# Two more expert pairs scattered, the last two summed in PSUM, low parts in pieces, and 512-column projections in a two-layer hybrid decoder kernel

## The chip, the cores and the metric

One core of a Trainium2 chip. The metric is the device time of one execution in microseconds (us), the median of three runs. TensorE (PE) multiplies matrices, VectorE (DVE), ScalarE (ACT) and GpSimd (POOL) work element by element, SyncE (SP) issues most DMA transfers. SBUF is the memory on the chip, PSUM the small one into which PE writes.

## What is computed

Two layers over 528 tokens (16 learned meta tokens and 512 of the input), 1024 features. Each layer has a mixer (four heads of a gated delta rule beside sparse attention with a token indexer), a residual norm, a mixture of experts (32 experts, two per token), and a second norm. Cut from the reference:

```python
for l in range(DEPTH):
    proj = h @ w_in[l]
    dq, dk, dv, dz, db, da, sq, sk, sv, iq, ik, iw = jnp.split(proj, SPLIT_POINTS, axis=-1)
    o_dn = deltanet_group(dq, dk, dv, dz, db, da, ...)       # short convolution of 4 taps on q, k, v first
    o_sa = dsa_group(sq, sk, sv, iq, ik, iw, ...)            # per query the top keys by the indexer
    mix = jnp.concatenate([o_dn, o_sa], axis=-1) @ w_out[l]
    h = layer_norm(DEEPNORM_ALPHA * h + mix, ln1_g[l], ln1_b[l])
    ffn = hier_moe(h, ...)                                   # top group of 4, then 2 of its 8 experts
    h = layer_norm(DEEPNORM_ALPHA * h + ffn, ln2_g[l], ln2_b[l])
```

where `hier_moe` sums, over a token's two experts, gate x (silu(t w1) * (t w3)) w2.

## The kernel before, in words

The order in which each engine issues its instructions is fixed ahead of the run by the framework's list scheduler, from the program and a model of its costs; `tc.issue_after(x)` only keeps an instruction behind x. So a change in one place can move instructions everywhere.

**Projections.** Activations and weights are split into a high and a low part, and a projection is high x high + low x high + high x low: 24 products of 128 weight columns each, accumulated in one PSUM bank. `project` (L314) does the tokens in two halves of 264 columns, or of 256 where the meta tokens are left out (`c0` = 16): the index queries of both layers, and in layer 1 the attention queries, the gates and the output projection. `between` runs after the first half. `weights` (L213) loads 512 KB, ACT copies the high part and POOL subtracts the low part (L186, 1024 columns; every other weight of the output projection on DVE). The low parts share a tag with four buffers, the high parts one with two.

**Convolution.** The first of four taps is on POOL (L513), the other three on DVE (L515). `att_values` copies transposed values on DVE (L900).

**Experts.** 16 pairs of experts, 64 rows for each expert. For each pair: `gather` (L1234, POOL) fetches its tokens' rows by an indirect DMA, `transpose_rows` (L1362) transposes them on PE (xtq) and scales them on ACT and DVE into xT, in two halves; `expert_hidden` (L1308) makes h in 32 products; `expert_out` (L1323) makes the output yp in two halves of 8 products in the banks of `po_` and `pa`. For pairs 0 to 11 (`SENT` = 12, L49), `gated_rows` stores gate x yp into yw (ACT one half, L1349, DVE the other, L1350), and POOL scatters its rows into the table ytab in device memory (L1481). yw shares the high parts' two buffers, so a store waits for the scatter of two pairs before. For pairs 12 to 15, `gated` (L1340) stores a high part yw (ACT) and a low part yl (DVE), and `combine` (L1377) places the rows by products with a 0/1 matrix G (two per half tile of 128 tokens) and adds them on DVE (L1397) to the residual h. `todo` and `advance` (L1399 to L1403) spread the combinations of pairs 12 to 14 over the pairs that follow; those of pair 15 are in the tail.

**Weights of the experts** are six transfers of 1 MB per pair on SP's queue (`load_pair`, L309).

**Tail.** At pair 15, behind the vectors of the second norm (lnw), `fetch_rows` (L1416) loads the table's rows (yr) into the buffers of `unit`. A branch for experts with more than 64 tokens follows (`tc.If`, L1501; not taken here). Behind it `norm_stats` (L1598) does for each tile: `merge_rows` (L1431: two adds of the table's rows to h on DVE, L1434), the combination of pair 15, with the sum for the mean (on DVE, L1395, or, in the mode "e", on ACT with h itself added by a product with the identity), then variance and norm.

## Time and profile before

| | us |
|---|---|
| median of three runs | 1503.27 (1502.39 to 1503.33) |
| profiled execution | 1504.99 |
| its span, first to last instruction | 1503.2 |
| PE busy | 1312.8 |
| DVE busy | 882.5 |
| POOL busy | 588.1 |
| ACT busy | 528.4 |
| mean granted TensorE clock | 0.937 of full speed |

Layer 0's mixer takes until about 476, its experts until 735, its tail until 775; layer 1's mixer until 1217, its experts until 1470, the tail to the end. Times in the profile count from the start of the span. A busy PE includes waiting inside a pipelined run of products; what an instruction costs PE is therefore read from one start to the next. An idle time in brackets names what the profile found to have come last.

### The profile page before, as it was taken

The numbers are of one execution on the slowest core, as the hardware profiler recorded it, in microseconds if no ns is written. First come the engines' busy times: TensorE is split into PE (matmuls) and PEld (weight loads), VectorE is DVE, ScalarE is ACT, GpSimd is POOL, SyncE is SP. The second block draws the span as 40 slices with busy tenths as digits, with TensorE's granted clock in tenths as the row PEclk, the third lists the DMA queues.
The fourth block names the chain that finished last, engine by engine and source line by source line (L and its number), as shares of the span: only waits on it lengthen the run. The fifth ranks groups of instructions, "written<-read, shape, count | busy, mean of one in ns | idle before, by whom it ended". The sixth has DMA issues, their size and how long they took to land. (4 is left out here: it accounts for less than half of the span.)

```text
span 1503.2 us, 25678 instructions
## 1 busy us (share of the span) xinstructions
PE 1312.8 (87%) x9592; PEld 958.3 (64%) x9592; DVE 882.5 (59%) x2151; ACT 528.4 (35%) x1385; POOL 588.1 (39%) x581
## 2 busy tenths in 40 slices
PE   7898998799996898779778989988999879978794
PEld 7898998787894332223368989988888733322231
DVE  5898999656446131113788888998573341311157
ACT  3454544245322222222134544442453222221212
POOL 3665497626013211210146664878340231211102
PEclk9999999869997999999889999999799989999997
DMA  5252133122626999999432521222236379999971
GB/s 174 79 183 75 53 91 89 62 72 110 260 82 254 406 409 359 410 410 380 154 108 73 186 73 60 79 70 66 100 140 253 106 299 410 409 409 410 409 305 56
DMA packets 103121, 305.59 MB, mean 203 GB/s; under 512 B 24248, under 2 KB 25352, under 8 KB 102992
## 3 DMA queue, kind: packets, MB, share of 16 engines
q1 hardware_dynamic: 88464, 274.11, 48.8%
q0 software_dynamic: 8608, 16.94, 3.1%
q10 hardware_dynamic: 5920, 12.85, 2.3%
q8 instruction: 77, 1.26, 0.3%
q14 instruction: 52, 0.43, 0.1%
HBM read 281.49 MB, written 30.10 MB: 207 GB/s over the span
## 5 line engine op out<-in xcount | busy, mean ns | idle before, releaser
L186 POOL TENSOR_TENSOR wl<-wr,wh 128x1024 fp32r<-128x1024 f32 (+1 forms) x74 | 183.3, 2477 | 227.1 <-ACT wh L186 191.0
L61 PE MATMUL h<-we,xT 128*64 128x512 f32 x1024 | 231.1, 595 | 0.2
L61 PE MATMUL pj<-hh,wh 128*128 128x264 f32 (+2 forms) x1056 | 172.4, 299 | 11.0 <-DVE hl L186 5.1
L61 PE MATMUL pj<-hl,wh 128*128 128x264 f32 (+2 forms) x1056 | 167.9, 294 | 0.0
L61 PEld LDWEIGHTS h<-we,xT 128*64 128x64 f32 x1024 | 72.1, 137 | 139.7 <-issue 131.8
L61 PE MATMUL pj<-hh,wl 128*128 128x264 f32 (+2 forms) x1056 | 158.7, 289 | 1.2 <-POOL wl L186 1.2
L61 PEld LDWEIGHTS pj<-hh,wh 128*128 128x128 f32 (+1 forms) x1056 | 148.5, 198 | 13.8 <-DVE hl L186 5.3
L61 PE MATMUL yp<-we,hidT 128*64 128x512 f32 x512 | 128.1, 633 | 25.8 <-ACT yw L1349 23.1
L61 PEld LDWEIGHTS pj<-hl,wh 128*128 128x128 f32 (+1 forms) x1056 | 147.2, 197 | 0.6 <-issue 0.4
L61 PEld LDWEIGHTS pj<-hh,wl 128*128 128x128 f32 (+1 forms) x1056 | 141.5, 192 | 1.5 <-POOL wl L186 1.4
L1236 POOL MEMSET xe<- 128x1024 f32 x32 | 30.5, 952 | 259.9 <-PE h L61 243.9
L1319 DVE SCALAR_TENSOR_TENSOR hid<-hid,h 128x256 f32<-128x256 f32 x32 | 13.5, 421 | 197.3 <-ACT hid L1318 197.3
L186 ACT CAST wh<-wr 128x1024 fp32r<-128x1024 f32 (+1 forms) x82 | 85.5, 1045 | 78.1 <-PE pj L61 27.6
L1318 ACT ACTIVATE hid<-h 128x256 f32<-128x256 f32 x32 | 12.3, 383 | 246.6 <-PE h L61 235.1
L1372 DVE TENSOR_SCALAR xT<-xtq,lcol 128x128 f32<-128x128 f32 x64 | 26.2, 410 | 114.4 <-ACT xT L1374 107.9
L1374 ACT ACTIVATE xT<-xtq,lcol 128x128 f32<-128x128 f32 x192 | 73.4, 455 | 55.8 <-PE xtq L1367 55.3
L61 PEld LDWEIGHTS yp<-we,hidT 128*64 128x64 f32 x512 | 33.7, 142 | 89.1 <-issue 52.9
L515 DVE SCALAR_TENSOR_TENSOR dn<-cin,cw,dn 128x528 f32<-128x528 f32 x72 | 77.8, 1083 | 5.0 <-POOL dn L513 4.2
L490 DVE MATCH_REPLACE8 scores<-top,scores 128x272 f32<-128x272 f32 (+3 forms) x128 | 62.0, 487 | 0.0
L489 DVE MAX8 top<-scores 128x8 f32<-128x272 f32 (+3 forms) x128 | 60.6, 494 | 0.1
L513 POOL TENSOR_SCALAR dn<-cin,cw 128x528 f32<-128x528 f32 x24 | 47.8, 1990 | 8.7 <-ACT cin L332 8.7
L61 PE MATMUL cmb<-yw,G 128*128 128x512 f32 (+1 forms) x96 | 37.3, 511 | 14.8 <-DVE sums L1395 7.2
(436 smaller groups left out, 2661.5 us busy)
## 6 DMA issues: line engine op xcount, KB each, us to landing
we<-w SPq DMA_DIRECT2D x190, 1024.0 KB
wr<-w_in SPq DMA_DIRECT2D x64, 512.0 KB
wr<-w_out SPq DMA_DIRECT2D x16, 512.0 KB
yr<-ytab SPq DMA_DIRECT2D x16, 512.0 KB
ytab<-zr ACTq DMA_DIRECT2D x16, 264.0 KB
hu<-x SPq DMA_DIRECT2D x8, 512.0 KB
hs<-hu ACTq DMA_DIRECT2D x8, 512.0 KB
ytab<-zr ACTq DMA_DIRECT2D x16, 256.0 KB
```

Of the source, the lines that this page charges most:

```text
L61: return nc.tensor.matmul(out, lhsT=lhsT, rhs=rhs, start=start, stop=stop)
L186: return nc.scalar.copy(hi, src), lo_engine.tensor_tensor(lo, src, hi, op=OP.subtract)
L489: nc.vector.max(top, sc)
L490: nc.vector.match_replace(out=sc, in_to_replace=top, in_values=sc, imm_value=GONE)
L513: nc.gpsimd.tensor_scalar(dst, cin[:, 0:T], cw[:, ci:ci + 1], None, op0=OP.mult)
L515: nc.vector.scalar_tensor_tensor(dst, cin[:, j:j + T], cw[:, ci + j:ci + j + 1], dst, op0=OP.mult, op1=OP.add)
L1236: nc.gpsimd.memset(xe, 0.0)
L1318: nc.scalar.activation(hid, p1[:n, 0:2 * P], AF.Tanh, scale=0.5)
L1319: nc.vector.scalar_tensor_tensor(hid, hid, 1.0, p1[:n, 0:2 * P], op0=OP.add, op1=OP.mult)
L1372: last = nc.vector.tensor_scalar(xT[:, kk, :], src, g_, b_, op0=OP.mult, op1=OP.add)
L1374: nc.scalar.activation(xT[:, kk, :], src, AF.Identity, bias=b_, scale=g_)
```

## The change

- `SENT` goes from 12 to 14: pairs 12 and 13 are scattered into the table as well. Pairs 14 and 15 are kept with their G (`late`), and `combine` sums the products of both in PSUM, in the tail; `todo` and `advance` are gone. yw of pairs 14 and 15 holds both parts in a buffer of `unit`.
- At pair 15 `fetch_rows` comes ahead of the norm's vectors, and `merge_rows` is called there: two tiles behind pair 14's products, the others behind pair 15's hidden products; no longer in `norm_stats`.
- `weights`: POOL makes the low part in four pieces of 256 columns.
- `project`: as few products as 512 columns allow, so one of 512 where there were two of 256; `between` then runs behind the whole.
- The first tap and the copy of `att_values` go to ACT.

```diff
-SENT = 12
+SENT = 14
...
-        split(hi[:, :KT * m], lo[:, :KT * m], raw, nc.vector if src == "w_out" and ct % 2 else nc.gpsimd)
+        nc.scalar.copy(hi[:, :KT * m], raw)
+
+        eng, n = (nc.vector, 1) if src == "w_out" and ct % 2 else (nc.gpsimd, 4)
+        for i in range(n):
+            c = slice(i * KT * m // n, (i + 1) * KT * m // n)
+            eng.tensor_tensor(lo[:, c], raw[:, c], hi[:, c], op=OP.subtract)
...
-            w = (T - c0) // 2
-            for half in range(2):
+            n = -(-(T - c0) // 512)
+            w = (T - c0) // n
+            for half in range(n):
...
-                nc.gpsimd.tensor_scalar(dst, cin[:, 0:T], cw[:, ci:ci + 1], None, op0=OP.mult)
+                nc.scalar.activation(dst, cin[:, 0:T], AF.Copy, scale=cw[:, ci:ci + 1])
...
-            nc.vector.tensor_copy(vk[:, :, j * P:(j + 1) * P], p.rearrange("p (t c) -> p t c", t=4))
+            nc.scalar.copy(vk[:, :, j * P:(j + 1) * P], p.rearrange("p (t c) -> p t c", t=4))
...
-        def combine(t, j, G, yh, yl, last=None):
+        def combine(t, j, sets, last=None):
...
-                _mm(nc, p, g_, yh[j], start=last != "e", stop=False)
-                _mm(nc, p, g_, yl[j], start=False, stop=True)
+                for G, yh, yl in sets:
+                    for y in (yh, yl):
+                        _mm(nc, p, G[:, OFF[t] - q0:OFF[t] - q0 + P], y[j], start=first, stop=(G is sets[-1][0] and y is yl))
+                        first = False
...
-        todo = []
-
-        def advance(k):
-            for _ in range(min(k, len(todo))):
-                combine(*todo.pop(0))
...
-            yw = wpool.tile([P, D], F32 if pair < SENT else F32R, name="yw", tag="wh", bufs=2)
+            yw = (wpool.tile([P, D], F32, name="yw", tag="wh", bufs=2) if pair < SENT else unit("yw", F32R))
             load_pair(pair)
             if pair == 15:
...
+                fetch_rows()
...
-                fetch_rows()
+                with tc.issue_after(fed.ins):
+                    for t in norder[:2]:
+                        merge_rows(t)
             ws = wts.pop(pair)
-            if pair == 15 and l + 1 == DEPTH:
-                advance(10)
             hid, fed = expert_hidden(xT, ws[:4])
...
-            with tc.issue_after(fed.ins):
-                advance(5)
+            if pair == 15:
+                with tc.issue_after(fed.ins):
+                    for t in norder[2:]:
+                        merge_rows(t)
...
-            yh = [yw[:, 0:512], yw[:, 512:D]]
-            yl = halves("yl", "t")
+            yh, yl = ([yw[:, i + 512 * j:i + 512 * j + 512] for j in range(2)] for i in (0, D))
             done = gated(p3, gate, yh, yl)
-            with tc.issue_after(fed.ins):
-                advance(10)
-            G = slots(tki[:, pair:pair + 1])
-            last_pair = (G, yh, yl)
-            if pair < 15:
-                todo += [(t, j, G, yh, yl) for t in tiles_q for j in range(2 if t else 1)]
+            late.append((slots(tki[:, pair:pair + 1]), yh, yl))
...
-            merge_rows(t)
             for j in range(2 if t else 1):
-                combine(t, j, *last_pair, evac)
+                combine(t, j, late, evac)
```

How this moves instructions, at three places. PE in layer 1, from pair 13's output product on, before (hidT is the transposition of the hidden values, h_14432 pair 14's first product, cmb the combinations):

```order
L1329 MATMUL hidT<-cst,hid 128x128 x2
L1367 MATMUL xtq<-cst,xe 128x128 x4
L61 MATMUL yp_14371<-we_14322,hidT 64x512 x4
L1367 MATMUL xtq<-cst,xe 128x128 x4
L61 MATMUL cmb<-yw,G 128x512 x3
L61 MATMUL cmb<-yl,G 128x512 x2
L61 MATMUL yp_14370<-we_14320,hidT 64x512 x4
L61 MATMUL cmb<-yl,G 128x512
L61 MATMUL h_14432<-we_14420,xT 64x512 x4
L61 MATMUL h_14432<-we_14422,xT 64x512 x4
L61 MATMUL cmb<-yw,G 128x512
L61 MATMUL cmb<-yl,G 128x512
```

and now:

```order
L1335 MATMUL hidT<-cst,hid 128x128 x2
L1373 MATMUL xtq<-cst,xe 128x128 x4
L61 MATMUL yp_13829<-we_13799,hidT 64x512 x4
L61 MATMUL yp_13830<-we_13801,hidT 64x512 x4
L1373 MATMUL xtq<-cst,xe 128x128 x4
L61 MATMUL h_13876<-we_13864,xT 64x512 x4
L61 MATMUL h_13876<-we_13866,xT 64x512 x4
```

The combinations are gone from the stage, and both halves of the output product stand together, ahead of the second transposition. Pairs 7 to 12 keep the order of before, a transposition between the halves.

ACT at the same place, before (yp_14269 and yp_14270 are pair 12's output, yp_14370 and yp_14371 pair 13's):

```order
L1331 COPY hidT<-hidT 128x256
L1374 ACTIVATE xT<-xtq,lcol 128x128 x6
L1344 ACTIVATE yw<-yp_14269,gtab 128x512
L1344 ACTIVATE yw<-yp_14270,gtab 128x512
L1344 ACTIVATE yw<-yp_14370,gtab 128x512
L1344 ACTIVATE yw<-yp_14371,gtab 128x512
```

and now (yp_13673, yp_13751 and yp_13829 are outputs of pairs 11, 12 and 13):

```order
L1355 ACTIVATE yw<-yp_13673,gtab 128x512
L1355 ACTIVATE yw<-yp_13751,gtab 128x512
L1324 ACTIVATE hid<-h_13803 128x256
L1337 COPY hidT<-hidT 128x256
L1380 ACTIVATE xT<-xtq,lcol 128x128 x3
L1355 ACTIVATE yw<-yp_13829,gtab 128x512
L1380 ACTIVATE xT<-xtq,lcol 128x128 x3
```

Pair 13's store now stands between the two halves of pair 14's xT. POOL issues the scatters of pairs 10 to 13 one behind the other, after the last gather; before, those of pairs 10 and 11 stood there.

DVE at the end of layer 1's experts, before (hu are the tiles of h; the branch lies between the two pieces):

```order
L1345 SCALAR_TENSOR_TENSOR yl<-yp_14613,gtab,yw 128x512
L1397 TENSOR_TENSOR hu_12412<-hu_12412,cmb 128x512
L1345 SCALAR_TENSOR_TENSOR yl<-yp_14614,gtab,yw 128x512
L1397 TENSOR_TENSOR hu_12412<-hu_12412,cmb 128x512
L1305 TENSOR_LOAD nxi
```

```order
L1501 UNCONDITIONAL_BRANCH
L1434 TENSOR_TENSOR hu_12411<-hu_12411,yr_14543 128x1024
L1434 TENSOR_TENSOR hu_12412<-hu_12412,yr_14546 128x1024
L1434 TENSOR_TENSOR hu_12411<-hu_12411,yr_14549 128x1024
L1434 TENSOR_TENSOR hu_12412<-hu_12412,yr_14552 128x1024
```

and now:

```order
L1351 SCALAR_TENSOR_TENSOR yw<-yp_13999,gtab,yw 128x512
L1441 TENSOR_TENSOR hu_12089<-hu_12089,yr_13951 128x1024
L1351 SCALAR_TENSOR_TENSOR yw<-yp_14000,gtab,yw 128x512
L1441 TENSOR_TENSOR hu_12089<-hu_12089,yr_13951 128x1024
L1441 TENSOR_TENSOR hu_12090<-hu_12090,yr_13954 128x1024 x2
L1441 TENSOR_TENSOR hu_12089<-hu_12089,yr_13957 128x1024 x2
L1441 TENSOR_TENSOR hu_12090<-hu_12090,yr_13960 128x1024 x2
L1311 TENSOR_LOAD nxi
```

The adds of the table stand around the last store and ahead of the branch; they are still behind everything else of pair 15. In layer 0 it is the same, with the two adds of the meta tile among them.

## Rows read from the trace of the kernel before

**Rows 1.** The page's first part: busy time of the engines in us, their share of the span, and instructions.

```profile
PE 1312.8 (87%) x9592; PEld 958.3 (64%) x9592; DVE 882.5 (59%) x2151; ACT 528.4 (35%) x1385; POOL 588.1 (39%) x581
```

**Rows 2.** The page's second part, 40 slices of 37.6 us: GB/s that the DMA engines moved.

```profile
GB/s 174 79 183 75 53 91 89 62 72 110 260 82 254 406 409 359 410 410 380 154 108 73 186 73 60 79 70 66 100 140 253 106 299 410 409 409 410 409 305 56
```

**Rows 3.** Two windows of 50 us in layer 0's mixer, and the sum of seven from 25 to 375. Columns: busy time of PE, PE's weight loads, DVE, ACT and POOL, each with the number of instructions, granted clock, DMA share, GB/s.

```profile
175.00:225.00 50.00, 48.66 (x400) 47.15 (x399) 50.00 (x157) 22.37 (x81) 41.71 (x49) 1.00 0.30 87
...
275.00:325.00 50.00, 41.97 (x479) 39.63 (x479) 24.96 (x72) 14.39 (x41) 17.86 (x28) 0.76 0.26 87
...
sum 350.00, PE 326.16 PEld 307.40 DVE 287.29 ACT 160.28 POOL 216.51; mean PE 46.59 PEld 43.91 DVE 41.04 ACT 22.90 POOL 30.93
```

**Rows 4.** The same of layer 1's mixer, one window and the sum of seven from 775 to 1125.

```profile
1025.00:1075.00 50.00, 43.80 (x492) 40.36 (x490) 32.82 (x78) 15.45 (x41) 27.32 (x31) 0.79 0.15 47
...
sum 350.00, PE 328.03 PEld 308.44 DVE 293.57 ACT 157.81 POOL 212.33; mean PE 46.86 PEld 44.06 DVE 41.94 ACT 22.54 POOL 30.33
```

**Rows 5.** PE's timeline in pairs 2 and 3 of layer 1: start, length, instruction (h is a pair's first product, yp its output product).

```profile
1245.03 7.09 PE L61 MATMUL h<-we,xT 128*64 128x512 f32 x32
...
1254.46 3.65 PE L61 MATMUL yp<-we,hidT 128*64 128x512 f32 x16
...
1258.64 3.65 PE L61 MATMUL h<-we,xT 128*64 128x512 f32 x16
```

**Rows 6.** The same in pairs 12 and 13 of layer 1; in brackets the idle time before an instruction, with what ended it.

```profile
1399.50 7.04 PE L61 MATMUL h<-we,xT 128*64 128x512 f32 x32
...
1413.23 1.94 PE L61 MATMUL yp<-we,hidT 128*64 128x512 f32 x8 [1.82 <-ACT yw L1349]
1415.00 1.46 PE L61 MATMUL h<-we,xT 128*64 128x512 f32 x6
```

**Rows 7.** The same of pairs 14 and 15, layer 1.

```profile
1434.32 3.65 PE L61 MATMUL h<-we,xT 128*64 128x512 f32 x16
...
1451.52 1.07 PE L61 MATMUL h<-we,xT 128*64 128x512 f32 x2
...
1465.95 3.65 PE L61 MATMUL yp<-we,hidT 128*64 128x512 f32 x16
```

**Rows 8.** PE's timeline in layer 0, pair 13's first product and pair 15's output product.

```profile
674.31 7.04 PE L61 MATMUL h<-we,xT 128*64 128x512 f32 x32
...
728.99 3.65 PE L61 MATMUL yp<-we,hidT 128*64 128x512 f32 x16
```

**Rows 9.** POOL's timeline, the last two scatters of layer 1; and, from the view of the DMA issues between 1380 and 1475, the last two gathers with their time from issue to landing in us.

```profile
1409.40 1.01 POOL L1481 DMA_INDIRECT ytab<-yw,dest  x1 [0.30 <-issue]
1420.13 1.00 POOL L1481 DMA_INDIRECT ytab<-yw,dest  x1 [9.72 <-DMA ytab<-yw,dest]
...
xe<-hs,gix POOLq DMA_INDIRECT x2, 7.4
```

**Rows 10.** SP's DMA issues at the end of layer 1's experts: the table's rows.

```profile
1437.13 14.93 SPq L1423 DMA_DIRECT2D yr<-ytab  x8
```

**Rows 11.** DVE's timeline around the end of layer 1's experts: last store of pair 15, the eight adds of the table, first sum of the norm.

```profile
1470.92 0.74 DVE L1345 SCALAR_TENSOR_TENSOR yl<-yp,gtab,yw 128x512 fp32r<-128x512 f32 x1
...
1472.47 9.17 DVE L1434 TENSOR_TENSOR hu<-hu,yr 128x1024 f32<-128x1024 f32 x8 [0.21 <-DVEq L1501]
1481.56 0.68 DVE L1395 CUSTOM_DVE_ANT_0 hu<-hu,cmb 128x512 f32<-128x512 f32 x1
```

**Rows 12.** The same in layer 0: the first two adds, the first sum, and the last add, that of tile 4.

```profile
736.70 4.38 DVE L1434 TENSOR_TENSOR hu<-hu,yr 128x1024 f32<-128x1024 f32 x2 [0.21 <-DVEq L1501]
...
746.21 0.67 DVE L1395 CUSTOM_DVE_ANT_0 hu<-hu,cmb 128x512 f32<-128x512 f32 x1
...
758.32 3.31 DVE L1434 TENSOR_TENSOR hu<-hu,yr 128x1024 f32<-128x1024 f32 x1
```

**Rows 13.** PE's timeline in a projection of layer 0, eight products of 264 columns to a line.

```profile
100.53 1.14 PE L61 MATMUL pj<-hh,wl 128*128 128x264 f32 x8
101.50 1.13 PE L61 MATMUL pj<-hh,wh 128*128 128x264 f32 x8
```

**Rows 14.** From the two timelines, a tap on DVE and the low part on POOL that ran with it; then by instruction DVE's taps and POOL's low parts (duration in ns, min/median/max); then groups (busy us, mean ns, idle before with what ended it): DVE's taps, PE's products with the low parts, POOL's products of 64 x 256.

```profile
106.04 2.87 DVE L515 SCALAR_TENSOR_TENSOR dn<-cin,cw,dn 128x528 f32<-128x528 f32 x1
...
105.95 2.39 POOL L186 TENSOR_TENSOR wl<-wr,wh 128x1024 fp32r<-128x1024 f32 x1 [0.70 <-POOL nk L555]
...
L515 DVE SCALAR_TENSOR_TENSOR dn<-cin,cw,dn x72: 746/768/2916, 50.5 to 937.9; 128x528 f32<-128x528 f32 x72
...
L186 POOL TENSOR_TENSOR wl<-wr,wh x74: 2151/2392/5006, 13.8 to 1176.7; 128x1024 fp32r<-128x1024 f32 x72, 128x928 fp32r<-128x928 f32 x2
...
L515 DVE SCALAR_TENSOR_TENSOR dn<-cin,cw,dn 128x528 f32<-128x528 f32 x72 | 77.8, 1083 | 5.0 <-POOL dn L513 4.2
...
L61 PE MATMUL pj<-hh,wl 128*128 128x264 f32 x768 | 115.3, 289 | 1.2 <-POOL wl L186 1.2
...
L923 POOL TENSOR_TENSOR qs<-qT,qs 64x256 fp32r<-64x256 f32 x32 | 24.0, 751 | 2.0
```

**Rows 15.** Groups as in the last three rows above: the first tap on POOL; an ACT instruction over 528 columns; and who waited for DVE's copy at L900 (us, times).

```profile
L513 POOL TENSOR_SCALAR dn<-cin,cw 128x528 f32<-128x528 f32 x24 | 47.8, 1990 | 8.7 <-ACT cin L332 8.7
...
L518 ACT ACTIVATE cin<-dn 128x528 f32<-128x528 f32 x24 | 15.5, 645 | 46.7 <-DVE dn L515 40.7 <-DVE dn L664 5.9
...
  PE vtm L902: 9.7, 3
```

25 lines of the change are left out of this document (15 added, 10 removed).

## The prediction

> **What bounds the kernel now.** The page's first part comes first: TensorE (PE) is busy 1312.8 us of the 1503.2 of the span, VectorE (DVE) 882.5, GpSimd (POOL) 588.1 [rows 1]. That is an average over stages with different limits, so the slices are next: DMA stands near 410 GB/s only in two stretches, those of the experts [rows 2]. I then read each stage by itself.
>
> In the mixers PE idles 22 to 24 us of 350 in either layer (350 less its busy time in the sums); from 175 to 225 DVE has no idle time at all, and behind such stretches the granted clock is 0.76 and 0.79 [rows 3, 4]. Both engines are near their limit there.
>
> In the experts' stage PE runs through one pair of experts after another. Early pairs start 13.6 us apart (1245.03, 1258.64) [rows 5]; pairs 12 and 13 start 15.5 us apart, and PE idles 1.82 us in between for a store of ScalarE (ACT) that frees a PSUM bank [rows 6]. From pair 14 to pair 15 it is 17.2 us, since products of earlier pairs' results stand between their own, and the last output product starts at 1465.95 [rows 7]. Layer 0 ends the same way [rows 8].
>
> In the tails DVE is the limit. In layer 1 it stores the last result, then adds eight rows of the table in a run of 9.17 us, and only then comes the first sum for the norm, at 1481.56 [rows 11]. In layer 0 that sum is at 746.21, with the adds of one tile still behind it [rows 12].
>
> **The change part by part.** I compare the instant at which DVE starts the norm's sums.
>
> *Pairs 13 to 15, layer 1.* In the new order no product of earlier pairs stands in the stage, and pairs 13 to 15 issue both halves of the output product one behind the other, as the pairs that take 13.6 us do. Pair 13 starts at 1415.00 [rows 6], so pair 15 at 1442.2; its output product starts 9.4 us after it (1254.46 - 1245.03) [rows 5], at 1451.6 against 1465.95: 14.3 us earlier. DVE's last store ended 5.7 us after the start of that product (1470.92 + 0.74 - 1465.95) [rows 11]. That gives 1457.3; one add of 1.15 us (9.17 / 8) now stands between the two stores, and seven behind them: 1465.4 where the one add lies in DVE's wait between the stores, 1466.5 where it doesn't. I take the first, being the nearest to what DVE waited: sums from 1465.4, **-16.2 us**.
>
> *The rows must be there.* Two more scatters precede the loads of the table's rows, and each waits until the one before has landed: 10.7 us from the one at 1409.40 to that at 1420.13. The gathers, of the same size, land in 7.4 us [rows 9]. Between these I take 9 us: the scatter of pair 13 is issued at 1438 and lands at 1447; at 10.7 us it lands at 1452. Eight loads of 0.5 MB at 410 GB/s take 10.2 us, and I allow 4 us for issue and release: first row at 1452 to 1457, last at 1461 to 1466. DVE comes to the last pair of adds at 1463.1. So this just fits, and costs at most 3 us. Today the loads take 14.9 us to issue [rows 10], behind weights; then they run almost alone.
>
> *Pair 13's store* takes a buffer that scatter 11 must have left (1420.13 + 9 = 1429.1), and in the new order it stands on ACT ahead of the second half of pair 14's activations. PE wants that half 16 products into pair 14, 3.65 us after 1428.6 [rows 5], so at 1432.2; it comes at 1429.1 + 0.7 + 1.2 = 1431.0. I cost it at nothing, with those 16 products as cover; without them it is 2 us per layer.
>
> *Layer 0.* Pair 15 starts at 674.31 + 27.2 = 701.5, its output product at 710.9 against 728.99 [rows 8]: 18.1 us. The adds follow as above, with two short ones of 0.4 us: 710.9 + 5.7 + 8.1 + 0.8 = 725.5. Before, two of them took 4.38 us [rows 12], stretched beside POOL's low part of the next layer's weights. That part still falls there; I bound it by 0 and 2.5 us and take 0.6. Sums from 726.1: **-20.1 us**. The adds of the last tile, 3.31 us for the one [rows 12], leave the tail too: at 1.2 us each, their length where nothing disturbs them, **-2.4 us**.
>
> *Tails.* Two more products per half tile, 34 in all. Sixteen products of 512 columns take 3.65 us [rows 5], 0.23 each, twice that at half clock. DVE's sums and norms cover part of it. Bounds 0 and 15.6; I take a fifth, **+3.1 us**, since DVE is what ends the tails today.
>
> *512 columns.* 24 projections of 24 products. Eight products of 264 columns take 0.97 us [rows 13], so one of 256 some 0.118, one of 512 0.23: 24 x 24 x (2 x 0.118 - 0.23) = 3 us if all lies on PE's path, nothing if not. **-3 us**. What was issued between the halves now follows the whole; at the end of layer 1's output projection that is half a product later, 2.8 us, covered by the next projection except for the last. Bounds 0 and 2.8; taken at nothing, as the last chunk's work was issued behind both halves before.
>
> *First tap and one copy on ACT.* The tap costs POOL 2.0 us, 24 times; ACT does 528 columns in 0.65 us [rows 15] and is busy 160 of 350 us [rows 3], so it has room. PE waited 9.7 us in three cases behind DVE's copy [rows 15].
>
> *Low parts in four pieces.* A tap on DVE that takes 0.77 us by the median took 2.87 beside a low part of 2.39; the 72 taps have 1.083 us on average, 22 us of delay in all [rows 14]. A piece has no row: a quarter of 2.39 us is 0.60, the nearest shape (64 x 256) takes 0.75 [rows 14], so POOL loses 0 to 0.6 us per weight. The Trainium skill, page "SBUF — State Buffer", section "Who interferes with whom", has DVE's two-input instructions and GpSimd's reads share one port pair, held for a whole instruction; the tap's row agrees. By it a quarter of the length would leave a quarter of the delay, which would be 16 us less on DVE and put the sum some 9 us lower.
>
> For tap, copy and pieces together I take **-7 us**, a sixth of the 46 us that PE idles in both mixers [rows 3, 4]. Bounds: -22, half of that idle time, and +6, if the low parts cost PE 0.1 us more in 60 weights.
>
> **Sum.** -16.2 - 20.1 - 2.4 + 3.1 - 3 - 7 = -45.6. The profiled execution took 1504.99 us, 1.8 more than its span; less 45.6 it is 1459.4. It lies 1.7 above the median of the runs, 1503.27, so the predicted time is 1457.7, in round numbers **1458 us**.
>
> **Rivals.**
> - *The transfers set the pace.* Six weights of 1.05 MB per pair need 15.3 us at 410 GB/s [rows 2], more than 13.6; the stage lives on what was loaded ahead. If pairs 14 and 15 wait for their weights, 1.7 us each, and the rows come 3 us late, each layer loses 6 us: 1470. For it: two more scatters on a full DMA. Against it: the rows' loads, which stand behind all weights, were issued from 1437.13 [rows 10], and pair 15 needs its last weight only at 1453. 0.15.
> - *DVE's relief is worth more.* The -7 becomes -22: 1443. For it: the 22 us of delay in the taps alone. Against it: PE is busy 48.66 of the 50 us in which DVE is full [rows 3], so more can't be won there. 0.17. The Trainium skill's section named above would make this the case to expect.
> - *Slower: the low parts come late.* A low part has taken up to 5.0 us [rows 14], and four pieces can be held up four times. If they take 0.65 us more in each of 72 weights, and PE waits for the end of every one, that is 47 us in the place of the 7 won: 1458 + 7 + 47 = 1512. It decides from the point at which POOL and not PE's own work is last. Against it: PE now waits 1.2 us for low parts in 768 products [rows 14]. 0.03.
> - *The mixers' order loses.* The whole order is written anew; it may open waits in the mixers that take back 15 us, and the clock with them: 1473. 0.05.
>
> **How the numbers follow.** The forecast has 0.60, the rivals 0.40. The range takes the forecast's own bounds, 1443 to 1471 (tails, columns and mixers at their ends), the transfers, and most of DVE's relief: 1441 to 1474. What a measurement of this kernel can tell from no change is 0.2%, 3 us; all cases but the slow one, and a little of the last, lie far beyond: faster 0.95, same 0.02, slower 0.03.
>
> **What would show it.** In the changed profile, layer 1: the first product of pair 15 27.2 us behind that of pair 13, with no product of earlier pairs between; seven adds back to back behind the last store, and the first sum 50.4 us after pair 13's start (66.6 now). Layer 0: 51.8 us (71.9 now). Each mixer 5 us shorter. It is wrong if PE waits for weights or activations in pairs 14 and 15, if the adds wait more than 3 us for the rows, or if PE's idle time on low parts passes 10 us.

## The result, and the profile after

| | before | changed |
|---|---|---|
| median of four runs, us | 1502.83 | 1455.8 |
| profiled execution, us | 1504.99 | 1451.2 |
| its span, us | 1503.2 | 1449.4 |
| mean granted TensorE clock | 0.937 | 0.944 |

The ratio is 0.9677 (95% interval 0.9632 to 0.9722). One of the four runs of the changed kernel, 2495 us, was disturbed and is left out of the ratio; the other three took 1451.1, 1451.2 and 1460.4. The predicted 1458 lies 2 us above the median, which counts all four, and 7 above the 1451.2 that is the median of the three. The terms behind it do not fit as well as their sum, and most of what follows is about that.

The span is cut in each layer at three instants that any of the profiles gives: the first expert product, that of pair 13, and DVE's first sum for the second norm. Times in us, as predicted and as measured:

| stage | before | after | difference | predicted |
|---|---|---|---|---|
| layer 0, mixer | 476.0 | 458.1 | -17.9 | -5 |
| layer 0, pairs 0 to 13 | 198.3 | 200.1 | +1.7 | 0 |
| layer 0, pair 13 to first sum | 71.9 | 58.3 | -13.6 | -20.1 |
| layer 0's tail and layer 1's mixer | 470.9 | 452.9 | -18.0 | -5.9 |
| layer 1, pairs 0 to 13 | 197.9 | 204.3 | +6.4 | 0 |
| layer 1, pair 13 to first sum | 66.6 | 52.8 | -13.8 | -16.2 |
| layer 1, tail | 21.7 | 23.0 | +1.4 | +1.6 |
| span | 1503.2 | 1449.4 | -53.8 | -45.6 |

(The predicted tails, +3.1 for both layers, are put half to each; layer 0's half and the -2.4 of its tile 4 are in the fourth row.)

**The end of the experts.** PE's timeline of layer 1 from pair 13's first product on (start, length, instruction, in brackets the idle time before it with what ended it):

```profile
1373.60 7.44 PE L61 MATMUL h<-we,xT 128*64 128x512 f32 x32
...
1387.52 7.09 PE L61 MATMUL h<-we,xT 128*64 128x512 f32 x32
...
1401.07 7.09 PE L61 MATMUL h<-we,xT 128*64 128x512 f32 x32
...
1410.50 3.65 PE L61 MATMUL yp<-we,hidT 128*64 128x512 f32 x16 [0.52 <-ACT hidT L1337]
1424.27 3.75 PE L61 MATMUL cmb<-yw,G 128*128 128x512 f32 x8 [10.12 <-DVEq L1506]
```

Pairs 13, 14 and 15 start 13.92 and 13.55 us apart, where [rows 7] had 17.2 between the last two. The last output product starts 36.90 us after pair 13, as forecast (36.6). Then PE stands still for 10.12 us. What ends that is DVE's sequencer at the branch (L1506), behind DVE's adds:

```profile
1413.21 0.75 DVE L1351 SCALAR_TENSOR_TENSOR yw<-yp,gtab,yw 128x512 fp32r<-128x512 f32 x1 [3.71 <-ACT yw L1350]
1413.88 1.22 DVE L1441 TENSOR_TENSOR hu<-hu,yr 128x1024 f32<-128x1024 f32 x1
1415.01 0.74 DVE L1351 SCALAR_TENSOR_TENSOR yw<-yp,gtab,yw 128x512 fp32r<-128x512 f32 x1
1415.67 8.40 DVE L1441 TENSOR_TENSOR hu<-hu,yr 128x1024 f32<-128x1024 f32 x7
1426.35 0.69 DVE L1408 CUSTOM_DVE_ANT_0 hu<-hu,cmb 128x512 f32<-128x512 f32 x1 [2.29 <-PE cmb L61]
```

That is DVE's timeline, which answers to [rows 11]. One add between the stores and seven behind them, back to back, as forecast; they end at 1424.07. At 1424.27 PE passes the branch and makes the eight products of the first tile, four for each half, at a granted clock of 0.50, and DVE waits 2.29 us for the first four. Before, PE made its products behind the branch beside DVE's adds of [rows 11] (1472.47 to 1481.64), so they were hidden:

```profile
1472.46 0.47 PE L61 MATMUL cmb<-yw,G 128*128 128x512 f32 x1 [1.72 <-DVEq L1501]
```

In both kernels PE's wait ends with DVE's sequencer at the branch; the 10.12 us against 1.72 are the adds that now stand ahead of it.

Layer 0 (PE, then DVE) shows the same 2.29 us and two things more:

```profile
685.17 3.65 PE L61 MATMUL h<-we,xT 128*64 128x512 f32 x16
689.42 1.94 PE L61 MATMUL h<-we,xT 128*64 128x512 f32 x8 [0.60 <-DMA we<-w]
691.98 1.94 PE L61 MATMUL h<-we,xT 128*64 128x512 f32 x8 [0.62 <-DMA we<-w]
```

```profile
701.42 2.83 DVE L1441 TENSOR_TENSOR hu<-hu,yr 128x1024 f32<-128x1024 f32 x2
...
704.99 1.69 DVE L1441 TENSOR_TENSOR hu<-hu,yr 128x1024 f32<-128x1024 f32 x1
...
710.81 1.23 DVE L1441 TENSOR_TENSOR hu<-hu,yr 128x1024 f32<-128x1024 f32 x1 [0.93 <-DMA yr<-ytab]
712.94 1.23 DVE L1441 TENSOR_TENSOR hu<-hu,yr 128x1024 f32<-128x1024 f32 x1 [0.90 <-SPq L1506]
716.46 0.69 DVE L1408 CUSTOM_DVE_ANT_0 hu<-hu,cmb 128x512 f32<-128x512 f32 x1 [2.29 <-PE cmb L61]
```

Pair 15 waits twice for weights, and one add waits 0.93 us for rows of the table; what the 0.90 us before the last add are is less sure, since the view names SP's sequencer at the branch. SP's and POOL's timelines say why the rows are late and why other adds are long:

```profile
685.43 2.38 SPq L1430 DMA_DIRECT2D yr<-ytab  x4
689.36 13.26 SPq L1435 DMA_DIRECT2D lnwq<-ytab  x8
702.66 2.14 SPq L1430 DMA_DIRECT2D yr<-ytab  x4
```

```profile
701.58 5.63 POOL L226 TENSOR_TENSOR wl<-wr,wh 128x232 fp32r<-128x232 f32 x4 [19.19 <-ACTq L1506]
```

The last four row loads stand behind eight small loads that took SP 13.26 us to issue. POOL's low part, in its four pieces, runs from 701.58 to 707.21 beside the adds, of which two took 2.83 us together and one 1.69, against 1.20 in layer 1 (8.40 / 7).

**Scatters and rows of the table** came in time. The last scatters of layer 1 on POOL answer to [rows 9], the loads on SP to [rows 10]:

```profile
1376.17 0.99 POOL L1492 DMA_INDIRECT ytab<-yw,dest  x1 [8.46 <-ACT yw L1355]
1384.23 0.97 POOL L1492 DMA_INDIRECT ytab<-yw,dest  x1 [7.07 <-ACT xT L1380]
1392.40 0.97 POOL L1492 DMA_INDIRECT ytab<-yw,dest  x1 [7.20 <-DMA ytab<-yw,dest]
```

```profile
1399.73 3.91 SPq L1430 DMA_DIRECT2D yr<-ytab  x8
```

They are 8.1 us apart (9 had been taken), and the eight loads issue in 3.91 us instead of 14.93.

**The mixers.** From 25 to 375 us, layer 0, PE is busy 333.41 of 350 where it was 326.16 [rows 3], and the granted clock rose from 0.93 to 0.98. The columns are those of [rows 3]; the row of before comes first, that of the changed kernel second:

```profile
25.00:375.00 350.00, 326.16 (x2933) 307.40 (x2931) 287.29 (x723) 160.28 (x470) 216.51 (x229) 0.93 0.28 91
```

```profile
25.00:375.00 350.00, 333.41 (x3036) 308.78 (x3034) 276.74 (x769) 180.13 (x506) 221.06 (x313) 0.98 0.32 107
```

DVE lost 10.6 us of work and ACT took 19.9. Three groups of the page after (busy us, mean ns of one, idle time before with what ended it) answer to [rows 14]:

```profile
L226 POOL TENSOR_TENSOR wl<-wr,wh 128x256 fp32r<-128x256 f32 (+1 forms) x296 | 250.3, 876 | 224.6 <-ACT wh L221 182.4
...
L61 PE MATMUL pj<-hh,wl 128*128 128x264 f32 (+2 forms) x928 | 158.8, 305 | 0.0
...
L521 DVE SCALAR_TENSOR_TENSOR dn<-cin,cw,dn 128x528 f32<-128x528 f32 x72 | 64.0, 897 | 10.8 <-ACT dn L519 9.7
```

A tap has 897 ns where it had 1083. A piece of a low part takes 876 ns, so a weight has 3.50 us of pieces where the whole took 2.39 by its median; and PE waited 0.0 us for low parts.

To compare stages I split each into three: PE's idle time; PE's **clock loss**, its busy time times (1 - granted clock), summed over slices of 5 us; and the rest, PE's work at full clock.

| stage | before: idle, clock loss, rest | after: idle, clock loss, rest |
|---|---|---|
| layer 0, mixer | 46.5, 25.9, 403.6 | 40.2, 11.6, 406.2 |
| layer 0, pairs 0 to 13 | 30.2, 5.0, 163.1 | 30.3, 6.2, 163.6 |
| tail 0 and mixer 1 | 45.9, 26.4, 398.6 | 31.2, 24.4, 397.3 |
| layer 1, pairs 0 to 13 | 30.2, 5.0, 162.7 | 30.3, 10.5, 163.5 |

So the 17.9 us of layer 0's mixer are 6.3 of idle time and 14.3 of clock, less 2.6; the 18.0 of layer 1's are 14.7 of idle time, 2.0 of clock and 1.3. The +6.4 in layer 1's pairs is nearly all clock.

### The profile page after: what moved, and what is told of

It reads as the page before. It is cut to its first block, busy times and chain, and to the rows that moved or that the text cites. A ratio compares the mean times of both kernels' runs of the same rounds, so it can differ in the third digit from the quotient of the medians.

```text
span 1449.4 us, 24501 instructions
## 1 busy us (share of the span) xinstructions
PE 1270.5 (88%) x8920; PEld 908.1 (63%) x8920; DVE 788.2 (54%) x2088; ACT 544.1 (38%) x1385; POOL 597.4 (41%) x779
## 3 DMA queue, kind: packets, MB, share of 16 engines
q1 hardware_dynamic: 88464, 274.11, 49.9%
## 4 chain that ended last, share of the span: by engine, by line
PE 30%; DVE 7%; issue 5%; DMA 3%; ACT 3%; POOL 1%; SPq 1%; POOLq 0%; ACTq 0%; DVEq 0%; another core or an unknown queue 0%
PE pj L61 8%; PE h L61 7%; PE yp L61 4%; PE d L61 1%; PE po L987 1%; DMA ytab<-yw,dest 1%; PE lgp L61 1%; DVE dn L668 1%; PE ptp L979 1%; PE xtq L1373 1%; DVE dn L521 1%; PE y L61 1%; PE vp L61 1%; PE ix L61 1%; POOL wl L226 1%
## 5 line engine op out<-in xcount | busy, mean ns | idle before, releaser
L226 POOL TENSOR_TENSOR wl<-wr,wh 128x256 fp32r<-128x256 f32 (+1 forms) x296 | 250.3, 876 | 224.6 <-ACT wh L221 182.4
L61 PE MATMUL pj<-hh,wh 128*128 128x264 f32 (+2 forms) x928 | 165.3, 315 | 6.7 <-ACT raw L338 3.6
L61 PEld LDWEIGHTS pj<-hh,wh 128*128 128x128 f32 (+1 forms) x928 | 135.1, 197 | 13.4 <-ACT raw L338 4.1
L61 PEld LDWEIGHTS pj<-hl,wh 128*128 128x128 f32 (+1 forms) x928 | 136.2, 195 | 6.8 <-DVE rs L1624 1.1
L61 PEld LDWEIGHTS pj<-hh,wl 128*128 128x128 f32 (+1 forms) x928 | 131.9, 190 | 5.1 <-issue 0.4
L1325 DVE SCALAR_TENSOR_TENSOR hid<-hid,h 128x256 f32<-128x256 f32 x32 | 13.5, 421 | 212.4 <-ACT hid L1324 212.4
L1380 ACT ACTIVATE xT<-xtq,lcol 128x128 f32<-128x128 f32 x192 | 73.6, 456 | 58.9 <-PE xtq L1373 58.3
L1378 DVE TENSOR_SCALAR xT<-xtq,lcol 128x128 f32<-128x128 f32 x64 | 26.2, 410 | 119.3 <-ACT xT L1380 119.3
L521 DVE SCALAR_TENSOR_TENSOR dn<-cin,cw,dn 128x528 f32<-128x528 f32 x72 | 64.0, 897 | 10.8 <-ACT dn L519 9.7
L1492 POOL DMA_INDIRECT ytab<-yw,dest x28 | 28.2, 1008 | 88.4 <-ACT xT L1380 45.9
L496 DVE MATCH_REPLACE8 scores<-top,scores 128x144 f32<-128x144 f32 (+3 forms) x128 | 62.0, 487 | 0.0
L495 DVE MAX8 top<-scores 128x8 f32<-128x144 f32 (+3 forms) x128 | 60.5, 494 | 0.2
L1335 PE MATMUL hidT<-cst,hid 128*128 128x128 f32 x64 | 14.0, 300 | 39.7 <-DVE hid L1326 39.7
## 6 DMA issues: line engine op xcount, KB each, us to landing
yr<-ytab SPq DMA_DIRECT2D x16, 512.0 KB, 11.8
```

The source lines that it names most:

```text
L61: return nc.tensor.matmul(out, lhsT=lhsT, rhs=rhs, start=start, stop=stop)
L226: eng.tensor_tensor(lo[:, c], raw[:, c], hi[:, c], op=OP.subtract)
L495: nc.vector.max(top, sc)
L496: nc.vector.match_replace(out=sc, in_to_replace=top, in_values=sc, imm_value=GONE)
L521: nc.vector.scalar_tensor_tensor(dst, cin[:, j:j + T], cw[:, ci + j:ci + j + 1], dst, op0=OP.mult, op1=OP.add)
L1378: last = nc.vector.tensor_scalar(xT[:, kk, :], src, g_, b_, op0=OP.mult, op1=OP.add)
```

## The experiments

**Theories.** (A) The experts' ends come from the scatters and the sums in PSUM, and what was missed there is the wait behind the branch. (B) The mixers' gain comes from the low parts in pieces, through DVE. (C, its rival) It comes from tap and copy, or from the new order as a whole, or from the clock. In the tables of this section, "mixers" are the first and fourth stage above, "ends" the third and sixth, as layer 0 / layer 1.

**Four parts, one at a time, on the kernel before.**

a1_columns, projections in one piece:

```diff
-            w = (T - c0) // 2
-            for half in range(2):
+            n = -(-(T - c0) // 512)
+            w = (T - c0) // n
+            for half in range(n):
```

> The kernel before, with the 512-column products alone. Stage spans before: start to the first expert product of layer 0 476.0 us, first sum of layer 0's norm to the first expert product of layer 1 470.9 us; in the changed kernel 458.1 and 452.9, so 17.9 and 18.0 us less, where the prediction had about 5 each. My theory (the mixers gained because DVE no longer waits for POOL's low parts and taps) expects this alone to give 1 us in layer 0 (4 projections) and 2 in layer 1 (20): total -2 to -4 us, 1499 to 1501. The rival (fewer PE instructions and evictions are what shortened the mixers) expects -8 us or more in layer 1 alone. A third theory (any new order of the scheduler is worth +-10 us) expects a change of either sign without a relation to the products.

a2_pieces, the low part in pieces:

```diff
-        split(hi[:, :KT * m], lo[:, :KT * m], raw, nc.vector if src == "w_out" and ct % 2 else nc.gpsimd)
+        nc.scalar.copy(hi[:, :KT * m], raw)
+
+        eng, n = (nc.vector, 1) if src == "w_out" and ct % 2 else (nc.gpsimd, 4)
+        for i in range(n):
+            c = slice(i * KT * m // n, (i + 1) * KT * m // n)
+            eng.tensor_tensor(lo[:, c], raw[:, c], hi[:, c], op=OP.subtract)
```

> The kernel before, with the low parts in four pieces of 256 columns alone. The port theory expects most of the mixers' gain here: DVE's mean tap (1083 ns) under 950, and -10 to -25 us in total over the two mixers, 1478 to 1493. The rival 'slower: the low parts come late' expects PE's idle time on low parts to rise from 1.2 us to 10 or more and the total at or above 1503. If the tap on ACT is what freed DVE, this gives less than 8 us.

a3_tap_copy, first tap and copy on ACT:

```diff
-                nc.gpsimd.tensor_scalar(dst, cin[:, 0:T], cw[:, ci:ci + 1], None, op0=OP.mult)
+                nc.scalar.activation(dst, cin[:, 0:T], AF.Copy, scale=cw[:, ci:ci + 1])
...
-            nc.vector.tensor_copy(vk[:, :, j * P:(j + 1) * P], p.rearrange("p (t c) -> p t c", t=4))
+            nc.scalar.copy(vk[:, :, j * P:(j + 1) * P], p.rearrange("p (t c) -> p t c", t=4))
```

> The kernel before, with the first tap and the copy of att_values on ACT alone; low parts in one piece. If POOL's taps (24 of 2.0 us) delayed DVE as the low parts do, DVE's mean tap falls by a fifth and the mixers by 5 to 15 us together, 1488 to 1498. If the pieces are what matters, -3 to -6 us, from the 9.7 us that PE waited behind DVE's copy.

a4_experts, the experts' whole part (`SENT`, the sums in PSUM, the table's loads and adds at pair 15) and nothing else:

```diff
-SENT = 12
+SENT = 14
...
+                with tc.issue_after(fed.ins):
+                    for t in norder[:2]:
+                        merge_rows(t)
...
```

> The kernel before, with SENT = 14, the sums of pairs 14 and 15 in PSUM and the merges at pair 15; mixers as before. By the parts measured in the changed kernel (from pair 13's first product to the first sum 71.9 to 58.4 us in layer 0 and 66.6 to 52.8 in layer 1) it should take 27 us off, 1474 to 1478, with both mixers within 5 us of before (476.0 and 470.9, the latter less 1 to 3 us for the two adds that leave the tail). If the experts' pairs 8 to 12 in layer 1 (17.3 us each instead of 15.5 in the changed kernel's profile) are slowed by the two more scatters, they are slow here too; if by chance of the clock, 15.5 again.

| | median, us | ratio to before, same chip | mixers | ends | idle in the mixers |
|---|---|---|---|---|---|
| before | | | 476.0 / 470.9 | 71.9 / 66.6 | 46.5 / 45.9 |
| a1_columns | 1519.8 | 1.0074 (1.0031 to 1.0118) | 476.4 / 478.0 | 69.5 / 66.9 | 49.9 / 52.4 |
| a2_pieces | 1492.02 | 0.9896 (0.9842 to 0.995) | 464.6 / 461.1 | 71.1 / 66.6 | 40.1 / 37.7 |
| a3_tap_copy | 1521.01 | 1.0061 (1.0003 to 1.0119) | 478.7 / 474.0 | 72.6 / 66.6 | 49.1 / 47.4 |
| a4_experts | 1484.5 | 0.9838 (0.9784 to 0.9891) | 477.5 / 472.0 | 58.3 / 52.3 | 45.0 / 42.8 |
| changed | 1455.8 | 0.9677 (0.9632 to 0.9722) | 458.1 / 452.9 | 58.3 / 52.8 | 40.2 / 31.2 |

a4 gives the ends of the changed kernel to half a microsecond and leaves the mixers within 1.5 us of what they were: (A) holds for the gain. Of the mixers only the pieces gain by themselves; the columns make the kernel slower, and the tap and copy gain nothing (slower, just beyond the interval). The view of the waits of a1, layer 1's mixer (who, for whom, us, times, longest), has on top a wait that before does not show among its longest:

```profile
PE y L61 <- DVE scores L676: 10.4, 2, 6.8
```

The four changes of the ratio add up to -1.3%, all of it together gives -3.2%: **the parts do not add up**. The waits in a4 also say what the fourth stage holds: before, PE waits 7.2 us in layer 0's tail for DVE's sums (L1395). In a4 that wait is gone, and the idle time of the stage is 3.1 us less, so some of the fourth stage's gain comes from the experts' part and not from the mixer.

**Parts taken back out of the changed kernel.** b1_whole_low takes out the pieces (a2's diff reversed), b5_halves goes back to two halves (of 256 columns where there are 512), b6_tap_copy_back puts the tap on POOL and the copy on DVE again (a3's diff reversed).

```diff
-            n = -(-(T - c0) // 512)
-            w = (T - c0) // n
-            for half in range(n):
+            w = (T - c0) // 2
+            for half in range(2):
```

> The changed kernel with the low parts in one piece again. Stages of the changed kernel: first mixer 458.1, from layer 0's first sum to layer 1's first expert product 452.9. Alone on the kernel before, the pieces took 11.4 and 9.8 us off these two. If they are what shortened the mixers, this one has 470 to 476 and 463 to 471 and is 20 to 35 us slower than the changed kernel. If the order that came with all parts together is what counts, with the pieces only one of its parts, less than 10 us slower.

> The changed kernel with two products of 256 columns again. Alone on the kernel before, the 512 columns lost 7 us in layer 1, with PE waiting 10.4 us for DVE's scores. If that loss is theirs, this kernel is up to 8 us faster than the changed one; if the 512 columns pay off only where DVE is free to follow (pieces, tap on ACT), 3 to 8 us slower, most of it in layer 1's mixer (452.9 to 456 or more), layer 0's within 3 us of 458.1.

> The changed kernel with the first tap on POOL and the copy on DVE again. Alone on the kernel before, tap and copy on ACT lost 3 us in each mixer although DVE's mean tap fell to 879 ns. If POOL's 24 taps of 2 us hold DVE where the pieces no longer do, the mixers are 5 to 10 us longer here (463 to 468, 458 to 463) and DVE's mean tap rises above 917; if the loss of the run alone carries over, 3 us shorter each.

| | median, us | ratio to before, same chip | mixers | ends | idle in the mixers | clock loss there |
|---|---|---|---|---|---|---|
| b1_whole_low | 1498.72 | 0.9933 (0.9894 to 0.9971) | 478.6 / 474.0 | 58.3 / 54.0 | 48.7 / 50.3 | 26.2 / 26.2 |
| b5_halves | 1464.51 | 0.9719 (0.9648 to 0.979) | 462.2 / 460.7 | 56.4 / 52.3 | 37.3 / 38.9 | 19.4 / 18.8 |
| b6_tap_copy_back | 1479.05 | 0.9761 (0.9673 to 0.9848) | 479.6 / 461.4 | 55.2 / 52.7 | 48.8 / 41.0 | 27.7 / 21.1 |

The time of b1 is the median of ten runs; its stages are those of its profiled execution, 1487.73 us, the fastest of the ten. Without the pieces the whole gain in the mixers is gone, so (B) holds in that the pieces are needed. But it does not hold in its mechanism: DVE's taps, whose delay was to be the path, have these groups in a2, a3, b1 and b6 (four kernels, in that order):

```profile
L520 DVE SCALAR_TENSOR_TENSOR dn<-cin,cw,dn 128x528 f32<-128x528 f32 x72 | 66.0, 917 | 14.8 <-POOL dn L518 13.8
```

```profile
L515 DVE SCALAR_TENSOR_TENSOR dn<-cin,cw,dn 128x528 f32<-128x528 f32 x72 | 62.9, 879 | 16.9 <-ACT dn L513 15.9
```

```profile
L516 DVE SCALAR_TENSOR_TENSOR dn<-cin,cw,dn 128x528 f32<-128x528 f32 x72 | 67.8, 950 | 13.8 <-ACT dn L514 13.1
```

```profile
L521 DVE SCALAR_TENSOR_TENSOR dn<-cin,cw,dn 128x528 f32<-128x528 f32 x72 | 62.8, 875 | 4.9 <-POOL dn L519 3.8
```

The pieces alone (a2) bring the taps to 917 ns, under the 950 that the theory asked for. But a3 has shorter taps (879 ns) than the changed kernel (897), with whole low parts, and its mixers are 2.7 and 3.1 us longer than before; and b6, where taps above 917 had been expected, has the shortest of all (875), and longer mixers than the changed kernel. Nor do tap and copy explain it (rival C's first form): alone they gain nothing, while without them layer 0's mixer is at 479.6 again. PE's wait for DVE's scores in layer 1's mixer is 10.4 us in a1 and 13.5 in b1, against 2.0 in the changed kernel; but before, whose mixers are as long, has other waits on top (7.2 us for DVE's sums, 6.2 for the copy at L900). What is late differs with each order.

b5 and b6 are less clear than b1: the intervals of both ratios overlap that of the changed kernel. What stands out is idle time in the mixers, against 38.8 to 43.2 us in layer 0 and 31.2 to 32.1 in layer 1 where the changed kernel's order ran again (the runs below): b6 has 6 and 9 us more, b5 7 more in layer 1 and nothing more in layer 0.

**The adds behind the branch again.** b2_merge_behind is the changed kernel with `merge_rows` called in `norm_stats`, as before:

```diff
             if pair == 15:
...
-                with tc.issue_after(fed.ins):
-                    for t in norder[:2]:
-                        merge_rows(t)
...
-            if pair == 15:
-                with tc.issue_after(fed.ins):
-                    for t in norder[2:]:
-                        merge_rows(t)
...
+            merge_rows(t)
```

> The changed kernel with the table's adds behind the branch again, in the norm's steps, everything else as changed. In the changed kernel PE waited 10.1 us in front of the branch for DVE's adds and then did pair 14's and 15's products for the first tile in 3.75 us at half clock, DVE's first sum 2.29 us behind the last add. My theory (adds ahead of the branch stand in a row with PE's sums, adds behind it run beside them) expects the first sum 3 to 5 us earlier in each layer (58.3 to 54 and 52.8 to 48 us from pair 13's start), of which the adds that come later in the tail take back up to 3.5: total -1 to -6 us. The rival (the adds need their place at pair 15, where DVE is idle) expects the total +5 to +10.

Measured: 1449.14 us, ratio 0.9633 (0.9559 to 0.9708). The ends are 49.0 / 47.7, so 9.3 and 5.0 us shorter than in the changed kernel, and the tail of layer 1 is 0.7 longer. DVE's timeline at layer 1's end:

```profile
1420.85 5.77 DVE L1441 TENSOR_TENSOR hu<-hu,yr 128x1024 f32<-128x1024 f32 x5 [0.38 <-DMA lnw<-ln_g]
1426.54 0.68 DVE L1408 CUSTOM_DVE_ANT_0 hu<-hu,cmb 128x512 f32<-128x512 f32 x1
```

Five adds stand ahead of the first sum, the others between sums, and no wait for PE is left in front of that sum. The two intervals overlap, so the whole time would not tell this kernel from the changed one; the ends do. The wait behind the branch is shown, and this edit takes it away. It does more than that: of layer 1's 5.0 us the wait is 2.29, and the rest comes from the three adds that now stand behind the first sum and lengthen the tail by only 0.7.

**The same program again, and the clock.** d0_changed_again is the changed kernel, unaltered.

> The changed kernel once more, the same program. Splitting each stage's time into PE's idle time, what its busy time lost to the granted clock (busy time x (1 - granted clock), in windows of 5 us) and the rest, the experts' pairs 0 to 13 had 30.2 us of idle time and 163 of rest in every kernel so far, and 5.0 to 13.6 us of clock loss; layer 0's mixer lost 11.6 us to the clock in the changed kernel's profile and 21.0 in the run with the adds behind the branch, whose order in that mixer is the same. If the clock loss is chance, idle time and rest come out within 2 us of the changed kernel's in every stage here (mixer of layer 0: 40.2 and 406.2; between the layers: 31.2 and 397.3) while the clock losses differ from it by up to 10 us. If the changed kernel holds the clock by its order, 11.6 and 24.4 come again within 2 us.

Measured: 1460.91 us (1447.85 to 1465.84), ratio 0.9682 (0.9631 to 0.9733). The same order of instructions in layer 0's mixer, on every engine, was run with a profile in the changed kernel, in b2 and in d0: clock loss 11.6, 21.0 and 16.0 us, the mixer 458.1, 464.8 and 465.2. Two windows of the changed kernel, then of b2 (columns as above):

```profile
275.00:300.00 25.00, 23.03 (x387) 22.12 (x388) 5.99 (x13) 8.41 (x18) 10.91 (x22) 0.93 0.21 67
300.00:325.00 25.00, 24.91 (x204) 21.19 (x204) 20.52 (x91) 16.23 (x69) 13.70 (x26) 0.93 0.31 107
```

```profile
275.00:300.00 25.00, 22.50 (x334) 21.80 (x335) 5.41 (x12) 6.89 (x14) 11.10 (x23) 0.73 0.22 66
300.00:325.00 25.00, 24.75 (x212) 22.07 (x204) 14.71 (x65) 12.65 (x48) 7.19 (x15) 0.80 0.30 107
```

PE is as busy in both, at 0.93 of full clock in one and at 0.73 and 0.80 in the other (d0 has 0.73 and 0.80 too), each a mean over stretches at 2.4 and at 1.2 GHz. So 9.4 of the 14.3 us that layer 0 gained by the clock are within what one program does from run to run. Idle time and rest come back within 3 us, where 2 had been expected (43.2 and 406.0 in d0 against 40.2 and 406.2; in layer 1 32.1 and 396.8 against 31.2 and 397.3). The gain of idle time in layer 1 (14 to 15 us) therefore belongs to the program. That of layer 0 (3 to 8 us, with b2's 38.8) is about as large as the spread of its runs, 4.4 us, and the kernel before was profiled once, so it is likely but not shown. Of the clock's share it is not shown that it belongs to the program.

**Filling PE's gaps.** In the experts PE waits 1.4 us per pair for DVE's hid, and the idle time of pairs 0 to 13 is 30.2 to 30.5 us in every kernel with this order, while the clock loss is anywhere from 5.0 to 13.6. c2_warm puts 20 small products on constants, whose result nothing uses, behind each pair's hidden products:

```diff
+            with tc.issue_after(fed.ins):
+                warm(20, pc)
```

> The changed kernel with 20 products of 128 x 128 in bf16, whose result nobody reads, behind each pair's hidden product, where PE idles 1.4 us. They take some 1.1 us at full clock. If the clock falls in the experts' stage because of PE's gaps, the clock loss of pairs 0 to 13 is below 5 us in both layers (5.0 to 13.6 so far), and the stage 195 to 198 us in both. If the clock's falls there have another cause, 5 to 14 us again, and the stage 199 to 208.

Measured: 1459.91 us, ratio 0.9686 (0.9651 to 0.9721), as d0. The idle time fell to 15.3 in both layers; the clock loss stayed at 7.1 and 11.8. The idea that these gaps cost the clock falls.

The traces on record say where the clock goes instead. In every run pairs 1 to 3, 5 and 6 (counted from 0), whose one long gap is that before hidT (filled in c2), are at a granted clock of 1.00. Pairs 8 to 12 have a second gap, the 1.82 us of [rows 6], which c2 leaves as it is; at a clock of 1.00 such a pair takes 15.5 us, at 0.89 it takes 17.3. The clock is low right behind that second gap. In the changed kernel, layer 1, pair 11, the eight products take 3.15 us where [rows 6] had 1.94 (PE's timeline, then that stretch, columns as above):

```profile
1353.35 3.15 PE L61 MATMUL yp<-we,hidT 128*64 128x512 f32 x8 [1.82 <-ACT yw L1355]
```

```profile
1353.35:1356.27 2.92, 2.92 (x8) 0.82 (x10) 0.47 (x1) 0.00 (x0) 0.00 (x0) 0.60 1.04 410
```

The second gap alone does not decide it, since the kernel before has it at a clock of 1.00 in all these pairs. Why the clock falls behind it in some pairs and not in others stays open.

**The order of an early pair.** In the pairs that take 15.5 us, PE has the second half of the next pair's xtq between the two halves of the output product, and waits there for ACT's store (the 1.82 us of [rows 6]). b4_order keeps that half behind the whole output product of the pair before:

```diff
-        def transpose_rows(xe, xT):
+        def transpose_rows(xe, xT, behind=()):
...
+                with ExitStack() as s:
+                    for i in behind if j else ():
+                        s.enter_context(tc.issue_after(i.ins))
...
-            transpose_rows(xe, xT)
+            transpose_rows(xe, xT, outs)
```

> The changed kernel with one edit: the second transposition of a pair's rows stands behind both halves of the output product of the pair before, in all pairs. Pairs 7 to 12 take 15.5 us or more now, with PE idle 1.82 us in each for ACT's store of the pair before. If the order is what makes them longer than 13.6, the idle time in pairs 0 to 13 falls from 30.2 to some 19 us in each layer, the stage by 11 to 13 us, the total by 20 to 26. The rival from the prediction, that the transfers set the pace (six weights of 1.05 MB at 410 GB/s take 15.3 us), expects PE to wait for weights instead and the stage to keep 195 us or more.

Measured: 1450.72 us (1448.61 to 1452.36), ratio 0.9627 (0.9597 to 0.9658), 10 us below d0 on the same chip, where 20 to 26 had been expected; the two intervals overlap, and the stages tell the kernels apart. Pairs 0 to 13 take 190.9 / 187.5 us (201.6 / 204.7 in d0), the ends 65.3 / 63.5 (57.1 / 52.3): most of it is given back. In pairs 0 to 13 the idle time fell from 30.3 / 30.2 to 23.6 / 21.3 us (19 had been expected), but at the ends it rose from 19.3 / 14.9 to 25.4 / 21.9. What is left of the gain is about what the clock gave: without the second gap the granted clock is 1.00 in pairs 8 to 12 of both layers, here and in e1 below, and the clock loss of pairs 0 to 13 is 3.4 us in each layer, 4.6 and 7.0 under d0's. PE's timeline of layer 0, pairs 13 and 14:

```profile
653.51 1.94 PE L61 MATMUL h<-we,xT 128*64 128x512 f32 x8
656.09 1.94 PE L61 MATMUL h<-we,xT 128*64 128x512 f32 x8 [0.64 <-DMA we<-w]
659.45 1.94 PE L61 MATMUL h<-we,xT 128*64 128x512 f32 x8 [1.43 <-DMA we<-w]
662.01 1.94 PE L61 MATMUL h<-we,xT 128*64 128x512 f32 x8 [0.62 <-DMA we<-w]
...
670.87 1.94 PE L61 MATMUL h<-we,xT 128*64 128x512 f32 x8
```

Every eight products wait for their weight, 2.56 to 3.36 us apart, where 1.05 MB at 410 GB/s take 2.56; the two pairs start 17.4 us apart, where the early ones take 13.6. This is the rival "the transfers set the pace". It did not decide the changed kernel, where weights held up pairs 13 to 15 only by the 1.2 us in layer 0, and it decides here. That the slower early pairs gave the changed kernel time to load ahead is argued from these two, not shown by itself.

**Both edits.** e1_order_merge is the changed kernel with b4's and b2's edits.

> The changed kernel with both edits that shortened it: the second transposition behind the output product of the pair before, and the table's adds behind the branch. With the first alone the ends of the experts' stages (pair 13's first product to the first sum) were 65.3 and 63.5 us, and PE idled 12.6 and 10.1 us in front of the branch with the first sum 2.29 us behind the adds. The adds behind the branch took 9.3 and 5.1 us off these ends without it. If both add up, 56 to 60 us here, the total 8 to 13 us under the run with the order alone, 1438 to 1444 where the changed kernel takes 1456 to 1461. If the rows of the table, loaded behind the weights that now set the pace, come too late for it, the ends stay at 61 us or more and the total at 1446 or more.

Measured: 1439.93 us (1437.66 to 1445.54), ratio 0.9547 (0.9508 to 0.9587). Pairs 0 to 13 take 191.1 / 187.3, the ends 59.3 / 58.8, which is 6.0 and 4.7 less than with b4's edit alone. The total is 10.8 us under b4's, within the 8 to 13 expected: the two add up, and this version beats the kernel before and the changed one.

## Why the prediction was right, and where not

- **Pairs 13 to 15**: right. 27.1 us from pair 13 to pair 15 in layer 0 and 27.5 in layer 1 (27.2 forecast), no product of earlier pairs between, seven adds back to back in layer 1. Pair 13's store cost nothing, as taken: pair 14's 32 products in layer 1 run without a break (1387.52, 7.09 us). The sign of being wrong that PE waits for weights in pair 15 did show, but only in layer 0 and with 1.2 us.
- **The first sum**: the step failed that let DVE pass from the last add straight to the first sum. It was priced as in [rows 11], where PE's products behind the branch lay beside the adds. Moved ahead of the branch, the adds hold PE up there, and 2.29 us of PE, four products at a granted clock of 0.50, come behind them, in either layer. Layer 1: 36.90 + 13.57 to the end of the adds + 2.28 = 52.75, against 36.6 + 13.8 = 50.4. Layer 0: 38.15, since the weights held up pair 15 (1.2 us of waits on rows above), then 17.91 instead of 15.2 for stores and adds (the low part's pieces beside them, the late rows), then 2.29: 58.35 against 51.8. So -13.8 and -13.6 in the place of -16.2 and -20.1.
- **The rows of the table**: right in layer 1, with 8.1 us between scatters in place of 9. Layer 0's last four loads stand behind eight small ones, 13.26 us of SP's time, which the sum had left out (7.91 us before), and cost an add 0.93 us.
- **The tails**: +1.4 in layer 1 against +1.6.
- **512 columns, tap, copy and pieces**: the forecast's -10 became about -35 (the two mixers, less layer 0's tail), the term that was mis-sized by most. It was bounded by half the idle time, 22 us. Idle time gave 21.0 in both mixers together, some of it in layer 0's tail; the clock gave another 16, and the bounds had no term for it. The rival that DVE's relief is worth more had a size nearer to this, -22 for these parts, but not the cause, as the next points say. What the runs show is that idle time fell, that the pieces are needed for it (b1), that tap and copy gain nothing alone and save idle time beside the pieces in both mixers (a3, b6), and that the columns lose alone and save idle time beside the pieces in layer 1 only (a1, b5). What makes them work together stays open: each edit rewrites the whole order, and an experiment that holds the order and changes the instructions was not tried.
- **The low part's price**: a piece took 876 ns, so a weight takes 1.03 us more than in one piece (3.50 less 2.47, the whole's mean in b1, 183.1 us / 74), above the 0.6 given as the end and above the 0.65 from which the slower rival was to decide. It cost nothing since PE waited 0.0 us for low parts: the condition of that rival was rather whether POOL is last, and it isn't.
- **DVE's relief**: taps are 186 ns shorter, 13.4 us in 72. The pieces alone (a2) gave 12.0 of this and a longest tap of 1.24 us, where it was 2.92 before and still 2.90 with whole low parts in b1. The prediction's estimate by the rule of the Trainium skill ("SBUF — State Buffer", "Who interferes with whom") was 16; the trace agrees with the rule on the delay. It does not with the step from there to the time, since a3's taps are as short and its mixers are not.
- **Early pairs**: taken at nothing. +1.7 and +6.4, with idle time and rest as before: the clock. It is not the two more scatters, since a1, a2 and a3, whose experts are those of before, take 198.4 to 206.7 us here, and b1, whose experts are the changed ones, 198.4 and 199.6.

So the total came out near the forecast partly because errors cancel: against the forecast the ends gave 8.9 us less, the mixers 25 more, and 8 of those went back in the early pairs. By the two profiled executions the change is 8 us larger than forecast (53.8 against 45.6), by the medians 1.4 (47.0).

## What to carry to other kernels

Work that is moved ahead of a branch also delays what every other engine has behind it: ask what the slowest engine's successor will then have to do first, and leave work behind the branch to cover it. Here all of the adds were put back (b2); leaving only some there was not tried. A gain in a stretch where the clock moves should be split into idle time and clock, and the same program run again, before any of it is credited to the change. Before a gap is filled for the clock's sake, see behind which gap the clock is low. And a cadence of a stage is not its limit until one has seen which wait makes it: here 15.5 us were an order on PE, and the transfers' limit showed once it was mended.
